# Two layers of a diffusion backbone on one core: another pattern of filler in layer 0's attention, and the first norm's sums between the halves of a modulation chunk

## The chip, the cores and the metric

The kernel runs on one core of one Trainium2 chip. The metric is the device time of one execution in microseconds (us). The time before is 1468.76 us, the median of three runs (1468.34 to 1469.26).

## The reference, cut to what matters

Two layers work on 512 latent tokens and, in layer 0, on 256 context tokens too; the width is 1024. In fp32:

```
for l in range(2):
    m = silu(cond) @ w_mod[l] + b_mod[l]          # six vectors of 1024 per stream: shift, scale, gate, twice
    h = rmsnorm(x, norm1_g[l]) * (1 + sc1) + sh1
    z = h @ w_in[l]                                # q (8 heads), k, v (2 heads of 64), u, g
    attn: softmax(q k^T) v; context sees context, latents see context and latents
    gm  = gelu(u) * (w_spatial @ layernorm(gelu(g)) + b)      # per group of 128 channels, chunks of 128 tokens
    x = x + ga1 * (concat(attn, gm) @ w_out[l])
    h2 = rmsnorm(x, norm2_g[l]) * (1 + sc2) + sh2
    x = x + ga2 * (relu(h2 @ w_ff1[l])**2 @ w_ff2[l])
```

The output is the latent stream alone.

## The kernel before, in words

Matrix products keep fp32 accuracy by a split: each operand is a high part (ACT, a cast, L226 for weights) and a low part (DVE, the difference, L231), and a product is three matmuls (L222). Activations lie transposed, channels on partitions. Weights come through a ring of buffers; `block_order()` fixes the order in which SP issues their loads: for layer 0 the modulation blocks `w_mod` (chunks 0 to 3 at the start, 4 to 11 during the attention, where high and low parts lie ready in memory) and the `w_out` blocks in the order in which the filler uses them.

**The start.** `start()` is scheduled in program order on PE and DVE. It computes the sum of squares of the latents (`lat.step`, the accumulate L498), modulation chunk 0 (16 matmuls in the trace, L373, from four loaded tiles, two per half), then `lat.sums`: the sums over partitions by matmuls with ones (L507), the scaling (L510), the power on POOL (L317), and the diagonal matrix of the result (L529). `fins.pop()()` picks the chunk's values out of its transpose (L381) by a selection matmul (L386) and stores them as shift and scale (L449, L452). `lat.bcast` spreads the norm over partitions (L534). Then the first half of chunk 1, then pieces of the normed input (L522 on DVE, L523 on ACT, L524 low part on DVE) and the first projection's main matmuls (L222).

**Layer 0's attention.** 16 tiles of the context and 32 of the latents run through one pipeline: scores (PE into `pa`), their maximum (DVE, L1052), the exponential (ACT, L1057), transposes of the weights (L1068 into `pt`) and their split (ACT L1070, DVE L1071), products with the values (PE into `pb`), the scaling, and mixing with the denominators (L1095 to L1101). The spatial mixing's matmuls (`pt<-ws,e` and `pt<-ws,acc`, L222, ended by L947 and L952) run among the context's tiles. A scheduler with costs of its own orders the rows of each engine inside this region. With each tile's step one **filler** is offered to TensorE: first the four halves of modulation chunks 4 and 5, then what the string FILL0 says. An "m" is half of a modulation chunk of 6 to 11, four matmuls that each use 32 of the 128 columns, so that four run side by side (L373). An "o" is a piece of the output projection's part from the spatial mixing, 12 matmuls of 128x384 (L222, `pb<-A,hi` and `pb<-A,lo`); the first "o" makes its operands (`make_gm`: ACT L812, DVE L814). A "." leaves the step without filler. When FILL0 is used up, 8 pieces of the output projection's attention part for the context follow, then 8 for the latents; the latter wait until all of the latents' tiles are done.

Of the kernel before, what the change touches and what calls it, by code (L numbers as in the profile page):

```python
# [8 lines left out]
F32 = mybir.dt.float32  # L9
# [3 lines left out]
ALU = mybir.AluOpType  # L13
# [100 lines left out]

FILL0 = "mmoooooooomomom.mom.mom.mom.mo.oo"
AB = ["A7", "A6", "A5", "A4"], ["B1", "B2", "B3", "B4"]
EARLY = AB[0] + ["B0"] + AB[1] + ["B5"] + AB[0] + ["B6"] + AB[1] + ["C0"]
PLAN = (("w0", "kv", "x0", "u1", "u2", "u3", "A0", "A1", "A2", "q", "B0", "B1", "B2"),  # L120
# [3 lines left out]
def block_order():  # L124
# [3 lines left out]
    for l in range(DEPTH):  # L128
# [17 lines left out]
        if l == 0:  # L146
            o += mod(4) + mod(5)
            rest = mod(6) + mod(7) + mod(8) + mod(9) + mod(10) + mod(11)
            n = 0
            for c in FILL0:  # L150
                if c == "m":
# [20 lines left out]
def trunk(ctx: ExitStack, tc: tile.TileContext, xT, pk1, pk2, rope, wsT, w_mod, w_tok, w_u, w_out, w_ff1, w_ff2, outT):  # L172
    nc = tc.nc
    vec, act, pe, pool_e = nc.vector, nc.scalar, nc.tensor, nc.gpsimd
# [46 lines left out]
    def mm(out, a, b, start, stop, n):  # L221
        pe.matmul(out, a, b, start=start, stop=stop)  # L222
        fl.vt += max(n / 2.4, 113.0) + 3.0

    def split(hi, lo, src, eng=None):
        act.copy(hi, src)  # L226
        if state.get("gated") and eng is vec and src.shape[-1] == 1024:
            for c in (slice(0, 512), slice(512, 1024)):
                vec.tensor_tensor(out=lo[:, c], in0=src[:, c], in1=hi[:, c].bitcast(F32), op=ALU.subtract)  # L229
            return  # L230
        (eng or vec).tensor_tensor(out=lo, in0=src, in1=hi.bitcast(F32), op=ALU.subtract)  # L231
# [8 lines left out]
    held, pend = [], []  # L240

    def convert():

        if held:
            split(*held.pop(0))

    def pump():
        while state["live"] < RING and state["pos"] < len(order):
# [111 lines left out]
    fins, mods = [], []  # L360

    def mod_chunk(l, j, lag=1200.0):


        ps = pb()
        ns = 4
        rows = ns * 32
        for kb in range(0, 4, ns // 2):
            ws_ = take("mod", l, j, kb) if j > 3 else (take("mod", l, j, kb)[0], take("mod", l, j, kb + 1)[0])
            for k2 in range(ns):  # L370
                k = kb * 2 + k2
                q = k2 * 32
                pe.matmul(ps[q:q + 32, :], S32[:, k, :], ws_[k2 // 2][:, k2 % 2 * 512:(k2 % 2 + 1) * 512], start=k < ns, stop=k >= KT - ns)  # L373
            fl.vt += PAR["MV"] * ns
            if j > 3:
                release()
            if kb < 4 - ns // 2:
                yield

        tr = (tw if l == 0 and j < 4 else tsm)([128, 512])  # L380
        vec.transpose(tr[0:rows], ps[0:rows])  # L381

        def fin():
            p4 = pt((128, 4, 2))
            for a in range(4):
                pe.matmul(p4[a * 32:a * 32 + 32], P1("sel")[0:rows], tr[0:rows].rearrange("p (m a i) -> p a m i", m=4, a=4)[:, a, :, 0:2], start=True, stop=True)  # L386
            if l == 0 and 0 < j < 4:
                mods.append(lambda: mod_store(l, j, p4))
            else:
                mod_store(l, j, p4)  # L390
        if lag is None:
            fins.append(fin)
        elif lag:
            fl.defer(lag, fin)
        else:
            fin()
        yield
# [65 lines left out]
    cx = kv0 = None  # L463
# [8 lines left out]
    def run(gen):  # L472
        for _ in gen:
            fl.tick()
# [231 lines left out]
    def layer(l, h, nxt, K, kv=None, kv0=0):  # L706
# [562 lines left out]
        def mixed(a, b):  # L1269
            for c in FILL0:  # L1270
                if c == ".":
                    yield "wait"
                else:
                    next(a if c == "o" else b)
                    yield
            yield from a
            yield from b
# [184 lines left out]
    def start():  # L1462
        chunk = [mod_chunk(0, c, None) for c in range(4)]
        for k in range(KT):
            lat.step(k)
        run(chunk[0])
        lat.sums(pool=1)
        fins.pop()()
        lat.bcast()
        next(chunk[1])  # L1470
        kvq = WideProj(h0)
        for c in range(4):
            k = 2 * c
            if c:
                convert()
                mods.pop()()
            lows = [lat.pieces(h0, k)]
            if not c:
                convert()
                lows.pop()()  # L1480
            lows.append(lat.pieces(h0, k + 1))
            for f in lows:
                f()
            if c == 2:
                for i in range(KT):
                    cx.step(i)
            if 0 < c < 3:
                run(chunk[c + 1])
            kvq.latents(k, cx.sums if c == 3 else fins.pop() if fins else None)
            if not c:  # L1490
                run(chunk[1])
            kvq.latents(k + 1, fins.pop() if fins else None)
        cx.bcast()
        return kvq
# [4 lines left out]
    lat, cx = Norm(0, 0, 0, 512, 0), Norm(0, 0, 512, 256, 1)  # L1499
    h0 = [unit(f"A{k}", [128, 2, T]) for k in range(8)]  # L1500
    with tc.manual_schedule(engines={ET.PE, ET.DVE}):
        kvq = start()
    while held:
        convert()
    held = None
# [63 lines left out]
```

## Time and profile before

| | |
|---|---|
| median of three runs | 1468.76 us (1468.34 to 1469.26) |
| profiled execution | 1468.59 us, its span 1466.8 us |
| granted TensorE clock, mean | 0.999 |
| TensorE busy | 1435.3 us, 98% |
| VectorE, ScalarE, GpSimd busy | 913.5, 639.8, 354.0 us |
| HBM | 145.26 MB read, 100 GB/s over the span |

Engines: PE is TensorE, PEld its weight loads, DVE VectorE, ACT ScalarE, POOL GpSimd, SP SyncE, which issues the DMAs. A row of the timeline is start, duration, engine, line, operation, output<-inputs, shape and count; in brackets stand the idle time of the engine before it and what ended that. A row of waits is engine, output and line, what was waited for, the total in us, how often, and the longest. Where stretches are listed, the columns are from:to, length, busy time and count of each engine named, granted clock, DMA share and GB/s. Busy TensorE time is modelled from pipelined matmuls, so it isn't TensorE at its peak.

### The profile page before, as it was taken

The page shows a single profiled execution, that of the slowest core. Times are in us where ns is not written, and L with a number is a line of the kernel's source. Part 1 is how long each engine was busy: PE and PEld are TensorE (multiplying, and loading weights), DVE is VectorE, ACT ScalarE, POOL GpSimd, SP SyncE. Part 2 cuts the span into 40 slices and gives each one's busy share as a digit, 9 for nine tenths or more (in the row PEclk, how much of TensorE's full clock was granted, in tenths as well). Part 3 has the DMA queues.
Part 4 walks back from the last instruction along what each step waited for, and adds up shares of the span by engine and source line. Part 5 has one row for each costly group of instructions (what it writes and reads, how often), then busy time and mean ns, then how long its engine had stood idle before and what let it go on. Part 6 is the DMA issues. An engine that isn't in the chain of part 4 may idle for free.

```text
span 1466.8 us, 21050 instructions
## 1 busy us (share of the span) xinstructions
PE 1435.3 (98%) x8178; PEld 1224.1 (83%) x8178; DVE 913.5 (62%) x1613; ACT 639.8 (44%) x1134; POOL 354.0 (24%) x304
## 2 busy tenths in 40 slices
PE   6999999999999999999999999999999999999998
PEld 2899787988888888888888889998989888888887
DVE  5857767777766565655556537778868554444443
ACT  3552546664545453433424234547755223332221
POOL 0333512222256461323233223142221000000000
PEclk9999999999999999999999999999999999999999
DMA  9322544101233343434343212210002323332331
GB/s 368 115 73 87 192 150 143 65 1 58 85 128 119 108 145 97 142 97 131 104 144 110 92 43 74 101 59 30 30 29 80 122 88 100 101 98 90 101 101 58
DMA packets 50084, 148.72 MB, mean 101 GB/s; under 512 B 5440, under 2 KB 6976, under 8 KB 49984
## 3 DMA queue, kind: packets, MB, share of 16 engines
q1 hardware_dynamic: 49408, 146.72, 30.0%
q8 instruction: 64, 1.05, 0.3%
q10 hardware_dynamic: 576, 0.66, 0.1%
q14 instruction: 36, 0.29, 0.1%
HBM read 145.26 MB, written 2.10 MB: 100 GB/s over the span
## 4 chain that ended last, share of the span: by engine, by line
PE 89%; DVE 6%; ACT 2%; DMA 1%; issue 1%; POOL 1%; SPq 0%; POOLq 0%; ACTq 0%; DVEq 0%
PE pa L222 55%; PE pb L222 25%; PE pt L222 2%; PE pb L373 2%; PE pt L1068 2%; PE pt L1192 1%; PE pt L764 1%; DMA A<-in_w_mod 1%; ACT hi L226 1%; DVE s L545 1%; DMA hi<-in_w_mod 0%; DVE A L541 0%; POOL m L317 0%; DVE X L1002 0%; DVE lo L229 0%
## 5 line engine op out<-in xcount | busy, mean ns | idle before, releaser
L222 PE MATMUL pa<-A,hi 128*128 128x512 f32 (+2 forms) x1440 | 429.7, 376 | 0.5 <-ACT hi L226 0.3
L226 ACT CAST hi<-raw 128x1024 fp32r<-128x1024 f32 x168 | 176.0, 1048 | 328.2 <-PE pa L222 242.0
L222 PEld LDWEIGHTS pa<-A,hi 128*128 128x128 f32 x1440 | 262.7, 188 | 46.7 <-ACT hi L226 0.5
L222 PE MATMUL pa<-A,lo 128*128 128x512 f32 (+2 forms) x832 | 283.9, 347 | 0.0
L231 DVE TENSOR_TENSOR lo<-raw,hi 128x1024 fp32r<-128x1024 f32 x144 | 191.4, 1329 | 119.6 <-ACT hi L226 115.8
L422 POOL TENSOR_TENSOR C<-C,s 128x512 f32<-128x512 f32 x112 | 175.4, 1581 | 293.9 <-ACT s L421 287.1
L222 PE MATMUL pa<-B,hi 128*128 128x512 f32 x750 | 239.0, 391 | 0.0
L222 PEld LDWEIGHTS pa<-A,lo 128*128 128x128 f32 x832 | 156.6, 188 | 21.6 <-DVE lo L229 0.2
L1002 DVE SCALAR_TENSOR_TENSOR X<-pa,modT,X 128x512 f32<-128x512 f32 x168 | 99.8, 615 | 106.5 <-PE pa L222 105.1
L222 PEld LDWEIGHTS pa<-B,hi 128*128 128x128 f32 x750 | 139.9, 188 | 27.1
L222 PE MATMUL pb<-B,hi 128*128 128x512 f32 (+1 forms) x600 | 156.8, 349 | 0.8 <-DVE mix L1224 0.7
L222 PE MATMUL pa<-B,lo 128*128 128x512 f32 (+1 forms) x450 | 155.2, 354 | 0.0
L1002 DVE SCALAR_TENSOR_TENSOR X<-pb,modT,X 128x512 f32<-128x512 f32 (+3 forms) x116 | 70.8, 619 | 76.9 <-PE pb L222 76.7
L222 PE MATMUL pb<-hi,A 128*128 128x256 f32 (+1 forms) x608 | 118.1, 291 | 0.6 <-DVE m L744 0.6
L222 PEld LDWEIGHTS pb<-B,hi 128*128 128x128 f32 x600 | 104.4, 189 | 15.5 <-DVE X L1002 0.9
L222 PE MATMUL pb<-B,lo 128*128 128x512 f32 (+1 forms) x300 | 104.1, 347 | 0.0
L222 PEld LDWEIGHTS pb<-hi,A 128*128 128x128 f32 x608 | 96.9, 191 | 2.2 <-PE pb L222 0.8
L222 PEld LDWEIGHTS pa<-B,lo 128*128 128x128 f32 x450 | 84.5, 188 | 14.9
L421 ACT ACTIVATE s<-k,silu 128x512 f32<-128x512 f32 x112 | 77.8, 717 | 36.6 <-DMA k<-in_w_mod 29.5
L222 PE MATMUL pb<-lo,A 128*128 128x256 f32 (+1 forms) x304 | 87.7, 289 | 0.0
L222 PE MATMUL pb<-A,hi 128*128 128x384 f32 (+2 forms) x288 | 81.1, 362 | 0.4 <-DVE mix L1099 0.3
L1399 DVE TENSOR_TENSOR w<-pa,w 128x256 f32<-128x256 f32 x28 | 11.9, 425 | 89.0 <-ACT w L1398 89.0
(230 smaller groups left out, 2250.0 us busy)
## 6 DMA issues: line engine op xcount, KB each, us to landing
raw<-in_w_ff SPq DMA_DIRECT2D x128, 512.0 KB, 3.5
k<-in_w_mod SPq DMA_DIRECT2D x96, 256.0 KB, 2.9
raw<-in_w_tok SPq DMA_DIRECT2D x16, 512.0 KB, 3.5
raw<-in_w_out SPq DMA_DIRECT2D x16, 512.0 KB, 3.5
lo<-in_w_mod SPq DMA_DIRECT2D x16, 512.0 KB, 4.5
hi<-in_w_mod SPq DMA_DIRECT2D x16, 512.0 KB, 4.3
A<-in_w_mod SPq DMA_DIRECT2D x8, 512.0 KB, 10.1
B<-in_w_mod SPq DMA_DIRECT2D x8, 512.0 KB, 9.4
```

The source lines that it names most:

```text
L222: pe.matmul(out, a, b, start=start, stop=stop)
L226: act.copy(hi, src)
L231: (eng or vec).tensor_tensor(out=lo, in0=src, in1=hi.bitcast(F32), op=ALU.subtract)
L373: pe.matmul(ps[q:q + 32, :], S32[:, k, :], ws_[k2 // 2][:, k2 % 2 * 512:(k2 % 2 + 1) * 512], start=k < ns, stop=k >= KT - ns)
L421: act.activation(p, w, AF.Copy, scale=s)
L422: pool_e.tensor_tensor(out=a, in0=a, in1=p, op=ALU.add)
L545: vec.scalar_tensor_tensor(out=t, in0=xk(k)[:, off:off + n], scalar=Amod[l][w][:, k, cond:cond + 1], in1=self.bc[:, 0:n], op0=ALU.mult, op ...
L764: pe.transpose(p[:, o:o + 128], stk[:, t, hh, c0:c0 + 128].bitcast(F32), ident)
L1002: vec.scalar_tensor_tensor(out=xs, in0=src[:, s - off:e - off], scalar=modT[l][:, i * 8 + m, cond:cond + 1], in1=xs, op0=ALU.mult, op1=ALU ...
L1068: pe.transpose(tp_[:, (kt - k0) * 128:(kt - k0) * 128 + 128], p[:, kt * 128:kt * 128 + 128], ident)
L1192: pe.transpose(tp_[:, kt * 128:kt * 128 + 128], p[:, (k0 + kt) * 128:(k0 + kt) * 128 + 128], ident)
L1399: vec.tensor_tensor(out=c, in0=ps[:, 512:768], in1=c, op=ALU.add)
```

## The change

FILL0 gets a new pattern: four halves of modulation chunks in front in place of two, 12 "m" and 16 "o" as before, and 8 pauses in place of 5, which lie from the middle on. With it the order of the loads changes. At the start, the norm's sums stand between the two halves of chunk 0; the broadcast stands ahead of the selection; the first half of chunk 1 moves behind the first main matmuls (it is handed to the first projection step as what runs between its two token tiles); and the first block's low part is converted in two halves of 512 columns.

```
-FILL0 = "mmoooooooomomom.mom.mom.mom.mo.oo"
+FILL0 = "mmmmooooo.oomo.mo.m.mom.mo.mo.moo.oo"
...
+    def convert_first():
+
+        hi, lo, raw = held.pop(0)
+        act.copy(hi, raw)
+
+        def low(c):
+            vec.tensor_tensor(out=lo[:, c], in0=raw[:, c], in1=hi[:, c].bitcast(F32), op=ALU.subtract)
+        low(slice(0, 512))
+        return lambda: low(slice(512, 1024))
...
+        next(chunk[0])
+        lat.sums(pool=1)
         run(chunk[0])
-        lat.sums(pool=1)
+        lat.bcast()
         fins.pop()()
-        lat.bcast()
-        next(chunk[1])
         kvq = WideProj(h0)
...
             if not c:
-                convert()
+                later = convert_first()
                 lows.pop()()
             lows.append(lat.pieces(h0, k + 1))
+            if not c:
+                later()
...
-            kvq.latents(k, cx.sums if c == 3 else fins.pop() if fins else None)
+            kvq.latents(k, cx.sums if c == 3 else fins.pop() if fins else (lambda: next(chunk[1])) if not c else None)
```

In the changed kernel the lines behind `convert_first` have numbers larger by 10 (L373 is L383, L386 is L396, L507 is L517, L534 is L544, L1068 is L1078).

TensorE at the start of the program, before: chunk 0 (`pb<-A`), sums, selection, broadcast, chunk 1's first half (`pb<-B`), main matmuls.

```order
L373 MATMUL pb_208<-A_8_101,S_88 32x512 x2
L373 MATMUL pb_208<-A_9_103,S_88 32x512 x2
L507 MATMUL pt_219<-ones,acc_50_185 128x1 x4
L386 MATMUL pt_230<-w_217,c_70 32x8 x4
L534 MATMUL pt_237<-c_70,w_228 128x128 x4
L373 MATMUL pb_242<-B_13_109,S_88 32x512 x2
L373 MATMUL pb_242<-B_14_111,S_88 32x512 x2
L222 MATMUL pa_247<-hi_107,A_42_175 128x512
```

And in the change:

```order
L383 MATMUL pb_208<-A_7_99,S_88 32x512 x2
L517 MATMUL pt_213<-ones,acc_50_185 128x1 x4
L383 MATMUL pb_208<-A_8_101,S_88 32x512 x2
L383 MATMUL pb_208<-A_9_103,S_88 32x512 x2
L544 MATMUL pt_230<-c_70,w_222 128x128 x4
L396 MATMUL pt_235<-w_228,c_70 32x8 x4
L222 MATMUL pa_242<-hi_107,A_42_175 128x512
L222 MATMUL pa_242<-lo_108,A_42_175 128x512
L222 MATMUL pa_242<-hi_107,A_42_175 128x512 x2
L222 MATMUL pa_242<-lo_108,A_42_175 128x512
L222 MATMUL pa_242<-hi_107,A_42_175 128x512
L383 MATMUL pb_261<-B_13_109,S_88 32x512 x2
```

The sums moved ahead of the second half of chunk 0, the broadcast ahead of the selection, and chunk 1's half behind six main matmuls.

VectorE at the same place, before (L381 the transpose of chunk 0, L529 the diagonal):

```order
L381 STREAM_TRANSPOSE w_217<-pb_208 128x512
L510 TENSOR_SCALAR m_224<-pt_219 128x4
L529 COPY w_228<-m_226 128x512
L449 TENSOR_TENSOR modT_90<-pt_230,c_70 128x2x4
L452 SCALAR_TENSOR_TENSOR A_92<-modT_90,c_70 128x4
```

And in the change:

```order
L520 TENSOR_SCALAR m_218<-pt_213 128x4
L539 COPY w_222<-m_220 128x512
L391 STREAM_TRANSPOSE w_228<-pb_208 128x512
L459 TENSOR_TENSOR modT_90<-pt_235,c_70 128x2x4
L462 SCALAR_TENSOR_TENSOR A_92<-modT_90,c_70 128x4
```

The transpose now stands behind the diagonal.

TensorE among the context's tiles, before (L373 halves of modulation chunks, L1068 transposes, `pa<-B,B` scores):

```order
L222 MATMUL pa_1879<-B_98_480,B_117_566 128x256
L373 MATMUL pb_1886<-hi_1591,S_88 32x512 x2
L373 MATMUL pb_1886<-lo_1592,S_88 32x512 x2
L373 MATMUL pb_1886<-hi_1843,S_88 32x512
L1068 MATMUL pt_1874<-c_70,w_1860 128x128 x2
L386 MATMUL pt_1891<-s_1866,c_70 32x8 x4
```

And in the change:

```order
L222 MATMUL pa_1878<-B_98_481,B_117_567 128x256
L383 MATMUL pb_1885<-hi_1592,S_88 32x512
L1078 MATMUL pt_1873<-c_70,w_1861 128x128 x2
L383 MATMUL pb_1885<-hi_1592,S_88 32x512
L383 MATMUL pb_1885<-lo_1593,S_88 32x512 x2
L396 MATMUL pt_1890<-s_1867,c_70 32x8 x4
L222 MATMUL pa_1907<-B_97_480,B_117_567 128x256
L222 MATMUL pa_1907<-B_98_481,B_117_567 128x256
L383 MATMUL pb_1885<-hi_1844,S_88 32x512
L1078 MATMUL pt_1902<-c_70,w_1883 128x128 x2
```

A half whose first matmul stands apart from its other three is called split here. In the order of the whole attention 5 halves of 16 are split before (2 among the context's tiles, 3 among the latents'), and 9 in the change (4 and 5).

## The prediction

> **What bounds the kernel now.** I read the page first, then the busy time by stage, then the waits of the stage that changes, then the first 28 us instruction by instruction.
>
> ```profile
> PE 1435.3 (98%) x8178; PEld 1224.1 (83%) x8178; DVE 913.5 (62%) x1613; ACT 639.8 (44%) x1134; POOL 354.0 (24%) x304
> PE 89%; DVE 6%; ACT 2%; DMA 1%; issue 1%; POOL 1%; SPq 0%; POOLq 0%; ACTq 0%; DVEq 0%
> ```
>
> TensorE is busy for 98% of the span and is 89% of the chain that ended last. So the time is TensorE's own work plus its few holes, and a change counts by what it does to either. The busy time of TensorE by stage (us from:to, length, busy, matmuls, granted clock, DMA share, GB/s):
>
> ```profile
> 0.00:24.00 24.00, 10.08 (x46) 0.93 0.94 351
> 24.00:160.00 136.00, 134.76 (x918) 1.00 0.33 115
> 160.00:190.00 30.00, 26.36 (x202) 1.00 0.75 258
> 190.00:300.00 110.00, 110.00 (x777) 1.00 0.31 108
> 300.00:330.00 30.00, 28.19 (x216) 1.00 0.01 2
> 330.00:1467.00 1137.00, 1125.91 (x6030) 1.00 0.28 92
> ```
>
> The changed pattern orders 160 to 330: 160 to 190 are the context's attention tiles with their spatial mixing, 190 to 300 the latents' tiles with filler, 300 to 330 the last tiles. The holes there are 3.64, 0 and 1.81 us. Who ended them:
>
> ```profile
> PE pt L386 <- DVE s L947: 1.3, 1, 1.3
> PE pt L1068 <- DVE A L1071: 1.2, 2, 0.8
> PE pt L222 <- DVE acc L231: 1.2, 1, 1.2
> PE pb L222 <- ACT A L1070: 0.6, 2, 0.4
> PE pt L1068 <- DVE modT L456: 0.6, 1, 0.6
> PE pb L222 <- DVE mix L1099: 0.3, 1, 0.3
> PE pb L373 <- DMA hi<-in_w_mod: 0.2, 1, 0.2
> ```
>
> The L1071 and L1070 rows are the bare last tiles (1.8 us together); the other five are the context stage (3.6 us). So no edit of the filler can win more than 5.4 us, and whatever it adds to TensorE in the full middle is paid in full.
>
> **The change part by part.** First the **start**, whose order in the trace of before is:
>
> ```profile
> 12.12 5.33 PE L373 MATMUL pb<-A,S 128*32 128x512 f32 x16 [12.12 <-DMA A<-in_w_mod]
> 17.39 1.05 PE L507 MATMUL pt<-ones,acc 128*128 128x1 f32 x8
> 17.51 0.72 DVE L381 STREAM_TRANSPOSE w<-pb 128x512 f32<-128x512 f32 x1 [4.14 <-PE pb L373]
> 18.37 0.25 PE L386 MATMUL pt<-w,c 128*32 128x8 f32 x8
> 18.79 1.02 POOL L317 TENSOR_TENSOR m<-m,mhalf 128x4 f32<-128x4 f32 x1 [17.81 <-DVE m L510]
> 19.84 0.43 DVE L529 COPY w<-m 128x512 f32<-128x512 f32 x1 [1.20 <-POOL m L317]
> 20.18 0.16 DVE L449 TENSOR_TENSOR modT<-pt,c 128x8 f32<-128x8 f32 x1
> 20.38 0.17 DVE L452 SCALAR_TENSOR_TENSOR A<-modT,c 128x4 f32<-128x4 f32 x1
> 20.41 1.09 PE L534 MATMUL pt<-c,w 128*128 128x128 f32 x4 [1.80 <-DVE modT L449]
> 21.43 1.94 PE L373 MATMUL pb<-B,S 128*32 128x512 f32 x8
> 21.54 0.75 DVE L522 SCALAR_TENSOR_TENSOR s<-X,A,pt 128x512 f32<-128x512 f32 x1 [1.00 <-PE pt L534]
> 23.30 0.73 PE L222 MATMUL pa<-hi,A 128*128 128x512 f32 x1
> 26.63 1.07 PE L373 MATMUL pb<-B,S 128*32 128x512 f32 x8
> ```
>
> Before, the sums (L507) follow the whole chunk 0; the square root on POOL, the diagonal (L529) and the broadcast (L534) come last, and the first main matmul starts at 23.30, 1.76 after the first scaled piece (L522, 21.54). Now the sums come behind half the chunk, that is about 12.12 + 5.33/2 = 14.8. They took 1.05; so early, with the first chunk's 16 matmuls at 0.33 us each against 0.13 in the row at 26.63, I allow twice that: 16.9. From the end of the sums (18.44) to the end of the diagonal (20.27) it was 1.83, so the diagonal ends at 18.7. The other half chunk, 1.07 to 1.94, ends between 18.0 and 18.8; the transpose now stands behind the diagonal on DVE and ends at 0.72 after the later, 19.5. Selection 0.25, L449 0.16, L452 0.17 and about 0.2 of handovers give 20.3 for L522, plus 1.76 the first main matmul at 22.1: 1.2 us earlier. Bounds: 2.3 earlier if the sums keep 1.05 and all slides with them, 0 if the later second half eats it.
>
> But chunk 1's first half stood at 21.43, between broadcast and first main matmul, where TensorE waited for DVE and ACT in any case. It now stands inside the first projection step, with nothing to hide it: 8 matmuls, +1.07 by the row at 26.63. (The two DMAs that its buffers hold back come some 2 us later; the queue still has work, and TensorE's stage from 24 to 160 has only 1.24 us of holes of all kinds, so I put that at 0, at most 1.) The conversion in two halves lets the scaled piece's low part in between; it costs one more DVE start, hidden by ACT's part. 0.
>
> The half chunk also kept TensorE busy ahead of the main matmuls. The clock:
>
> ```profile
> 17.00:20.40 3.40, 1.62 (x18) 1.14 (x17) 1.41 (x5) 1.04 (x1) 1.02 (x1) 1.00 1.03 410
> 20.40:23.80 3.40, 3.38 (x13) 1.40 (x14) 2.40 (x4) 0.72 (x1) 0.00 (x0) 0.50 1.03 411
> ```
>
> A stretch with 1.62 of 3.40 us busy was followed by one at a granted 0.50, and the stretch of 3.38 busy by full clock. In the change 20.4 to 23.8 holds TensorE work from 22.1 only, 1.7 of 3.4, so I expect the next 3.4 us, all main matmuls, at 0.50. Eight matmuls took 1.94 there against 1.07, a loss of 45%: 3.4 x 0.45 = +1.5; at best 0, at worst a second part-stretch, 1.7 x 0.45 = 0.8 more. **Start: -1.2 + 1.07 + 1.5 = +1.4** (-1.2 to +4.4).
>
> The Trainium skill (TensorE: Matmul & The Clock Gate, Part 1: The HAM clock gate) says that the clock is halved by default, that about 3.4 us of sustained activity lift it, and that the window is free-running, so its phase differs from run to run. The stretches above agree on the length; that the phase differs no run shows yet. By that rule the loss here would be anything from 0 to 1.5 with the phase, the sum 1469.9 to 1471.4, and repeated runs of the change would scatter by it.
>
> **The filler: split halves.** Half a modulation chunk is four matmuls on four column groups (two of the high, two of the low part), each two records in the trace. Kept together, all four run side by side; where the scheduler puts other rows behind the first, it runs alone:
>
> ```profile
> 166.66 0.62 PE L373 MATMUL pb<-hi,S 128*32 128x512 f32 x2
> 167.66 0.51 PE L222 MATMUL pa<-B,B 128*128 128x256 f32 x2
> 210.74 1.04 PE L373 MATMUL pb<-hi,S 128*32 128x512 f32 x2
> 211.72 0.62 PE L222 MATMUL pb<-A,hi 128*128 128x384 f32 x2
> 215.18 0.62 PE L373 MATMUL pb<-hi,S 128*32 128x512 f32 x1
> 216.17 0.96 PE L222 MATMUL pa<-B,B 128*128 128x512 f32 x4
> ```
>
> A whole half takes 166.66 to 167.66, 1.00. A split one takes 210.74 to 211.72 and again 215.18 to 216.17: 0.98 + 0.99. So a split costs 0.97. In the order of before 5 halves are split, 2 in the context's stage and 3 among the latents; in the changed order 9, 4 and 5. **Context +1.94, latents +1.94.** The latter has no hole to hide in (110.00 of 110.00). Lower bound of the first: 0, if the singles only fill waits.
>
> **The context's waits.** With four halves in front and dense pieces later, the waits for L947 (1.3), the accumulate L231 (1.2), L456 and the mix lose their place, since DVE gains about 2 us on TensorE: -3.6 at most. New ones arise. The transposes behind the first split wait for the exponentials (I take 0.6, like the L456 row); those behind the accumulate take 0 to 0.9; and the first dense pieces now stand right behind the last spatial mix, whose product must still go through DVE:
>
> ```profile
> 187.44 0.69 DVE L952 TENSOR_TENSOR C<-s,C 128x512 f32<-128x512 f32 x1
> 189.08 1.83 DVE L814 TENSOR_TENSOR A<-C,A 128x768 fp32r<-128x768 f32 x2
> ```
>
> From product to usable low part that is 0.69 + 0.92 and ACT's copy between, against some single rows of scores, values and transposes as cover; I take 1.6 (0.5 to 3.3). New waits 2.6, so **-1.0** (-3.1 to +0.6).
>
> **Pauses and end.** Before, 37 fillers ran ahead of the 8 output pieces and the last three of 48 tiles were bare; now 40 do, and each of the last 8 tiles has a piece of 12 matmuls. That takes the 1.8 of L1071 and L1070: **-1.8** (at least -0.8, if half of it returns). The three new pauses leave tiles bare in the full middle; those before left no hole there, so **+0.3**, at most 1.5, the price of a bare tile or two at the end (0.8 each at the longest).
>
> Sum: 1.4 + 1.94 + 1.94 - 1.0 - 1.8 + 0.3 = **+2.8 us**. The profiled execution took 1468.59 (span 1466.8 and 1.8 around it), so **1471.4**; the median of the runs shown, 1468.76, is 0.17 above that execution, well under the uncertainty of a term.
>
> **Rivals.** (a) The clock doesn't drop: the start is then -1.2 + 1.07 and the sum +1.3, 1469.9. For it: broadcast and selection fall into the stretch too, and TensorE may count as busy. Against: the 1.62 row. (b) Faster, by one mechanism in the context's stage: TensorE's extra second there is just what DVE lacked, so no wait returns and the two splits run inside what were holes. Then 3.6 goes and the 1.94 is not paid: 0 + 1.94 - 3.6 - 1.8 + 0 with an even start = -3.5, 1465.1. It decides once the new waits stay under about 0.3 us in all. For it: all five waits there are on DVE or a load and none on TensorE's own rows; against: DVE is already busy for most of that stage, and the dense piece directly behind the mix. (c) DMA becomes the bound in front: each half takes two loads of this kind,
>
> ```profile
> hi<-in_w_mod SPq DMA_DIRECT2D x16, 512.0 KB, 4.3
> ```
>
> so 1 MB, 4 us at the stage's 258 GB/s, and eight halves now follow each other where six did; one of them already waited for a load. If one misses its place by three quarters of that, 3.1 is added: 1474.5. Against: that wait was 0.2 and the loads run ahead through dense work. (d) The splits don't cost what they did, since neighbours fill them: the sum without 3.9 is -1.1, 1467.5; the rows at 210.74 and 215.18 speak against it.
>
> **How the numbers follow.** The forecast (1469.9 to 1473.5 as its own range) has 0.55; (a) 0.15, (b) 0.12, (c) 0.08, (d) 0.10. A change below 0.2%, 2.9 us, can't be told from none here. Faster by more: (b), 0.12. Slower by more than 2.9: (c) and half of the forecast, whose middle lies at 2.8: 0.36. The rest, 0.52, is within. The range leaves out half of (b) below and the upper end of (c): 1466.0 to 1474.8.
>
> **What would show it.** Right: the first main matmul near 22, half a chunk within the first projection step, and a granted 0.50 over the main matmuls after 23.8; nine places with L373 alone for 0.97; the L947 and L231 waits gone and one before a 128x384 dense matmul on L812 or L814; no wait for L1071 or L1070 after 300. Wrong: TensorE's busy time from 160 to 330 not some 4 us larger, full clock at the start, or waits for w_mod loads over 1 us in the context's stage.

## The result and the profile after

The changed kernel takes 1477.96 us, the median of four runs (1475.83 to 1479.09), against 1468.55 for the kernel before on the same chip: a ratio of 1.006 (95% interval 1.0048 to 1.0073), 9.4 us slower. The prediction was 1471.4 with a range to 1474.8. The profiled execution took 1476.86, its span 1475.0. Where an execution ran in the chip's slower state, as one of the eleven of e7_cover_dve did (1776.71 us at a granted clock of 0.754), it is left out of the medians below.

Where the time arises can be read from one and the same matmul in both traces. First the first filler of the attention, from the two timelines, before and after:

```profile
163.71 0.62 PE L373 MATMUL pb<-hi,S 128*32 128x512 f32 x2
```

```profile
166.12 0.62 PE L383 MATMUL pb<-hi,S 128*32 128x512 f32 x2
```

Then the first broadcast of the second norm, just behind the attention, as the group of its line (nanoseconds of one, first and last start):

```profile
L534 PE MATMUL pt<-c,w x2: 273/273/273, 339.2 to 339.3; 128*128 128x128 f32 x2
```

```profile
L544 PE MATMUL pt<-c,w x2: 272/272/272, 347.4 to 347.5; 128*128 128x128 f32 x2
```

So 2.4 us are lost before 166, 5.8 between there and 347, and the span as a whole is 8.2 longer: nothing more is lost behind the attention. (The medians differ by 9.4; the trace shows one execution.) The start of the changed kernel, TensorE alone:

```profile
15.06 1.87 PE L517 MATMUL pt<-ones,acc 128*128 128x1 f32 x8
16.86 1.93 PE L383 MATMUL pb<-A,S 128*32 128x512 f32 x8
18.82 1.11 PE L544 MATMUL pt<-c,w 128*128 128x128 f32 x4
22.18 0.79 PE L222 MATMUL pa<-hi,A 128*128 128x512 f32 x1 [2.03 <-ACT A L533]
25.04 1.94 PE L383 MATMUL pb<-B,S 128*32 128x512 f32 x8
26.91 0.80 PE L222 MATMUL pa<-hi,A 128*128 128x512 f32 x1
```

The first main matmul starts at 22.18 in place of 23.30, as forecast (22.1). But chunk 1's half takes 1.94 inside the projection, where 1.07 was expected, and the matmuls up to 27.9 run at that pace: 5.7 us at half speed and not 3.4. The column of the granted clock, which prints 1.00 here until the first change of the clock is recorded at 27.9, doesn't show it; the durations do.

The waits of TensorE between 160 and 345:

```profile
PE pb L222 <- DVE A L824: 2.1, 1, 2.1
PE pb L222 <- ACT A L822: 1.4, 1, 1.4
PE pb L383 <- DVE s L391: 1.4, 1, 1.4
PE pt L1078 <- ACT w L1067: 0.8, 2, 0.5
PE pt L1078 <- DVE A L1081: 0.7, 1, 0.7
PE pb L222 <- POOL B L231: 0.2, 1, 0.2
```

The old holes (L947, L231, L456, L1099) are gone, as forecast, and new ones of 5.7 us stand in their place among the context's tiles where 3.6 stood; the last two rows are the end, 0.9 in place of 1.8. Behind the three largest stand GpSimd, VectorE beside it, and a load. First the two scalings of before, then the rows of the changed kernel:

```profile
179.32 1.11 DVE L922 TENSOR_SCALAR s<-s,mv,m 128x128 f32<-128x128 f32 x4
```

```profile
180.18 4.68 POOL L231 TENSOR_TENSOR lo<-raw,hi 128x1024 fp32r<-128x1024 f32 x2
181.29 3.66 DVE L932 TENSOR_SCALAR s<-s,mv,m 128x128 f32<-128x128 f32 x2
184.87 0.70 DVE L391 STREAM_TRANSPOSE s<-pb 128x512 f32<-128x512 f32 x1
193.97 1.05 ACT L226 CAST hi<-raw 128x1024 fp32r<-128x1024 f32 x1 [2.43 <-DMA raw<-in_w_out]
195.09 2.35 POOL L231 TENSOR_TENSOR lo<-raw,hi 128x1024 fp32r<-128x1024 f32 x1 [4.40 <-ACT hi L226]
195.78 3.35 DVE L824 TENSOR_TENSOR A<-C,A 128x768 fp32r<-128x768 f32 x2 [0.85 <-ACT A L822]
```

GpSimd takes the low part of a `w_out` block in 2.35 us. Two scalings of 128x128 on VectorE, where four took 1.11 us before, take 3.66 and end 0.1 us after GpSimd's two conversions (184.86). The dense pieces' two low parts, 1.83 in the row quoted in the prediction, take 3.35; the first alone takes 2.48 and ends 0.8 us after GpSimd's conversion, which is about its own length (0.92). TensorE waits for both: through the transpose behind the scalings (L391), and directly for the low parts.

ACT's wait of 1.4 us comes from a load. ACT had nothing to do for 2.43 us, until a `w_out` block landed; it cast the block from 193.97 on and came to the dense operands (L822) at 194.92, though they had been ready since 193.85 (the end of L962 on VectorE). The load of this block, the third, was issued at 187.57, with six halves' `w_mod` loads of FILL0 in front of it. In the kernel before there are three in front, and it was issued 14 us earlier:

```profile
173.29 1.50 SPq L273 DMA_DIRECT2D raw<-in_w_out  x2
```

The same late load sets GpSimd's conversion at 195.09, beside the low parts.

And the clock, in stretches of 3.4 us:

```profile
191.70:195.10 3.40, 2.67 (x27) 1.00 0.85 309
195.10:198.50 3.40, 0.63 (x2) 1.00 0.16 60
198.60:201.90 3.30, 3.30 (x14) 0.50 0.46 146
```

After the stretch with 0.63 us of work the next 3.4 are granted half speed: by the prediction's 45%, an estimated 1.5 us more.

### The profile page after: what moved, and what is told of

It reads as the page before. It is cut to its first block, busy times and chain, and to the rows that moved or that the text cites. A ratio compares the mean times of both kernels' runs of the same rounds, so it can differ in the third digit from the quotient of the medians.

```text
span 1475.0 us, 21057 instructions
## 1 busy us (share of the span) xinstructions
PE 1441.8 (98%) x8178; PEld 1227.4 (83%) x8178; DVE 919.7 (62%) x1614; ACT 640.6 (43%) x1134; POOL 354.0 (24%) x304
## 4 chain that ended last, share of the span: by engine, by line
PE 87%; DVE 7%; ACT 2%; issue 1%; POOL 1%; DMA 1%; SPq 0%; POOLq 0%; ACTq 0%; DVEq 0%
PE pa L222 55%; PE pb L222 23%; PE pt L222 2%; PE pb L383 2%; PE pt L1078 2%; PE pt L1202 1%; PE pt L774 1%; ACT hi L226 1%; POOL m L327 1%; DMA A<-in_w_mod 1%; DVE lo L231 0%; DVE s L555 0%; DMA lo<-in_w_mod 0%; DVE A L551 0%; DVE s L932 0%
## 5 line engine op out<-in xcount | busy, mean ns | idle before, releaser
L231 DVE TENSOR_TENSOR lo<-raw,hi 128x1024 fp32r<-128x1024 f32 x144 | 194.8, 1353 | 120.0 <-ACT hi L226 115.8
```

## The experiments

Each ratio is to the kernel before on the same chip.

**The start alone and the filler alone.** Two kernels, each with one part of the change.

```
e1_start: the changed kernel with FILL0 = "mmoooooooomomom.mom.mom.mom.mo.oo"
e2_fill:  the kernel before with FILL0 = "mmmmooooo.oomo.mo.m.mom.mo.mo.moo.oo"
```

> Only the start edit, the old FILL0. In the changed kernel's trace the first main matmul starts 1.1 us earlier, but a matmul of the first projection is 2.4 us later from 26 us on, and the clock is full only from 27.9. Clock theory (the quiet ahead of the main matmuls lets TensorE run them at half clock): +1 to +4 us against before, about +2.4, with runs that differ by up to 2 or 3 us. Rival, work only (the half chunk's 1.07 us against the 1.1 won, the clock of that one execution being chance): within 0.5 us of before. Either way the attention's holes stay those of before.

> Only the new FILL0, the old start. Theory (the two edits add up): +5.7 us against before, the difference that the changed kernel's trace gathers between 168 and 334 us: +3 by split halves, +2 by holes among the context's tiles, +1.5 by a stretch at half clock behind the holes, -0.9 at the end. Rival (the late start shifts loads against the attention and makes its holes): +1 to +3 us.

The start alone: 1470.68 us, 1.0013 (1.0005 to 1.0022), +2.2 by the medians. The filler alone: 1475.11, 1.0045 (1.0032 to 1.0058), +6.7. Together 8.9 of the 9.4: the parts add up, and the filler's loss doesn't hang on the start. In the trace of the start alone the first filler starts at 166.04, 2.3 us later than before; 0.6 of that lies ahead of everything that the edit moves, in the first load (first matmul at 12.75, before at 12.12). There half speed lay on 24.0 to 27.4, 3.4 us as forecast. In the filler's trace the holes are those of the changed kernel but for ACT's, 2.2 in place of 1.4, and the clock is lower for two stretches:

```profile
190.90:194.30 3.40, 1.17 (x9) 1.00 0.49 169
194.40:197.70 3.30, 1.22 (x5) 0.50 0.31 78
197.80:201.20 3.40, 3.40 (x15) 0.50 0.17 70
```

Two stretches with little work are followed by two at half speed here; in the changed kernel's execution it was one of each.

**The start with its cover.** Chunk 1's half goes back to where TensorE has nothing else to do.

```
 (e1_start)
         lat.bcast()
         fins.pop()()
+        next(chunk[1])
         kvq = WideProj(h0)
...
-            kvq.latents(k, cx.sums if c == 3 else fins.pop() if fins else (lambda: next(chunk[1])) if not c else None)
+            kvq.latents(k, cx.sums if c == 3 else fins.pop() if fins else None)
```

> The start edit with the old FILL0, but the first half of chunk 1 stands again between the selection and the first main matmul. Clock theory: TensorE stays busy there, the main matmuls get full clock about as early as before, and the 1.1 us from the sums stay: -1 us against before (-1.5 to 0), 3 us under the start edit. Rival, work only: the half chunk is out of the path again, so also -1; but then the start edit is at 0, and the two differ by 1 us.

1468.24 us, 0.9998 (0.9989 to 1.0007): 2.4 us under the start edit alone, where 1.07 of matmuls had been moved. In the traces the first filler starts at 162.00 here and at 166.04 there; of these 4.0 us 1.07 are the moved work and 0.55 the later first load, which leaves 2.4. So work only, which gave 1 us between the two, falls; the clock, which gave 3, holds.

```profile
19.06 1.77 PE L383 MATMUL pb<-B,S 128*32 128x512 f32 x8
21.25 0.50 PE L222 MATMUL pa<-hi,A 128*128 128x512 f32 x1 [0.42 <-ACT A L533]
24.53 1.07 PE L383 MATMUL pb<-B,S 128*32 128x512 f32 x8
```

The main matmuls start at 21.25, at full speed (0.50 for one, 1.07 for the half chunk). But 1 us faster than before was expected, and 0.2 came. That is only partly explained. In this execution (1467.24) the first filler starts 1.7 us earlier than before, and the granted clock of the context's stage, 160 to 190, is 0.94 against 1.00 before. The four kernels traced with the early sums and the old front (e1, e3, e7, e10) all show 0.89 to 0.94 there, and the four traced with the old start and the old front (before, e5, e6, e9) 1.00. Why was not tried.

**VectorE in place of GpSimd.**

```
 (e2_fill)
-            eng = pool_e if "%s%d" % key[:2] in PAR["WP"] and key[:3] != ("out", 1, 0) else vec
+            eng = pool_e if "%s%d" % key[:2] in PAR["WP"] and key[:3] not in (("out", 1, 0), ("out", 0, 0)) else vec
```

> The new FILL0 with the old start, and the low parts of the four w_out blocks of the dense pieces taken on VectorE in place of GpSimd. 7 split halves in place of 9 by the order, worth -1.9 us. Port theory (VectorE's instructions with two inputs in SBUF wait until GpSimd's 2.35 us conversions end; that makes the 1.4 and 2.1 us holes and, by them, the half-clock stretch): those holes and the stretch go, -4 to -5 us more, so about 6 us under the new FILL0 alone and near before. Rival (the holes come from the dense piece standing right behind the mix, whoever converts): only the -1.9, or worse by the 1.2 us that each conversion adds on VectorE.

1469.68 us, 1.0008 (0.9999 to 1.0017): 5.4 under the filler alone, 6 expected. Of the waits of this kernel the largest and the two for the dense operands, and then the two groups of VectorE that had been stretched:

```profile
PE pt L1068 <- ACT w L1057: 1.9, 4, 0.8
PE pb L222 <- ACT A L812: 0.6, 1, 0.6
PE pb L222 <- DVE A L814: 0.6, 1, 0.6
```

```profile
181.41 0.58 DVE L922 TENSOR_SCALAR s<-s,mv,m 128x128 f32<-128x128 f32 x2
191.95 1.82 DVE L814 TENSOR_TENSOR A<-C,A 128x768 fp32r<-128x768 f32 x2
```

The two scalings take 0.58 and the two low parts 1.82; the wait for L381 is gone. Of the 5.4 us about 2 go to two split halves fewer (L373's busy time falls from 25.76 to 23.53), the rest to the holes and the clock behind them. That GpSimd's conversions stretch VectorE's instructions holds. Not all that was expected came: the wait for the exponentials (L1057) grew from 0.8 to 1.9, and the half clock did not go, but fell from 6.8 us to 3.4:

```profile
190.00:300.00 110.00, 108.44 (x740) 0.98 0.29 98
```

The edit also moved a load: the third `w_out` block was issued at 181.30, with the filler alone at 185.01, and its cast ran at 186.84, long before the dense operands. So ACT's wait, 2.2 with the filler alone and 0.6 here, fell with the earlier load; how much of the gain is the load's and how much VectorE's this run doesn't separate.

**Split halves.** The first matmul of each half is handed out one filler earlier.

```
 (the kernel before, mod_chunk, for chunks 6 to 11)
+                if apart and k2 == 0:
+                    yield
 (mixed, behind each filler)
+                if FILL0[i + 1:i + 2] == "m":
+                    next(b)
```

> The kernel before, with the first matmul of each half of chunks 6 to 11 handed out one filler earlier than the other three: 12 split halves in place of 5 by the order, nothing else meant to change. Split theory (a lone matmul takes 0.97 us and TensorE is full there): +6.8 us, 0.97 for each of the 7. Rival (the neighbours run beside it or the time is found again in a later wait): less than +2.

1474.48 us, 1.0041 (1.0027 to 1.0055): +6.2 for 7 splits, 0.89 each, and no new stretch at half clock in its trace. L373's busy time within 160 to 345, before and with the halves apart (then, for the changed kernel, L383's):

```profile
160.00:345.00 185.00, 22.22 (x128) 1.00 0.32 109
```

```profile
160.00:345.00 185.00, 28.28 (x128) 1.00 0.32 108
```

```profile
160.00:345.00 185.00, 25.75 (x128) 0.99 0.31 107
```

The same 128 matmuls take 22.22, 28.28 and 25.75. The change's four further splits cost 3.5.

**Pauses alone and front alone.**

```
e6_pauses: the kernel before with FILL0 = "mmoooooooomo.mom.mo.m.mom.mo.m.mo.oo"
e11_front: the kernel before with FILL0 = "mmmmooooooomo.mo.m.mom.mo.momoooo"
```

> The kernel before with three more pauses from the middle on and its old front (two halves, then dense pieces): FILL0 = mmoooooooomo.mom.mo.m.mom.mo.m.mo.oo. 8 split halves in place of 5 by the order, +2.9; the waits at the bare last tiles fall from 1.8 to about 0.7, -1.1. Theory (the front makes the new holes, the pauses only the splits): +1.8 us, no waits for the dense pieces' operands and no half clock in the latents' stage. Rival (the pauses in the middle make the holes): +4 or more.

> The kernel before with the new front alone: FILL0 = mmmmooooooomo.mo.m.mom.mo.momoooo, 5 pauses as before and the last three tiles bare as before; 6 split halves in place of 5. Theory (the front makes the holes and the half clock): the waits for the dense pieces' operands (2 x 2 us) and for L381 (1.4) are there, +2 by holes, +1.5 to +3 by the clock, +1 by the split: +4.5 to +6. Rival (the new pauses make them): +1 to +2.

Pauses: 1470.94 us, 1.0018 (1.0008 to 1.0027), +2.7 where 1.8 was expected, and none of the new holes; L373's busy time rose by 3.0 (25.24 for 22.22), which covers the loss. Front: 1473.39, 1.0035 (1.0021 to 1.0048), +4.9, with them all:

```profile
PE pb L222 <- ACT A L812: 3.2, 1, 3.2
PE pb L222 <- DVE A L814: 1.8, 1, 1.8
PE pb L373 <- DVE s L381: 1.4, 1, 1.4
```

So the front makes the holes, the pauses don't.

**Two combinations that don't beat the kernel before.** The kept half and VectorE's conversion, with the old and with the new FILL0.

```
e7_cover_dve:     e3_cover with the line of e4_dve
e8_cover_dve_new: the same with FILL0 = "mmmmooooo.oomo.mo.m.mom.mo.mo.moo.oo"
```

> The old FILL0, the early sums with chunk 1's half kept ahead of the main matmuls, and the w_out low parts of the dense pieces on VectorE. 5 split halves as before. If the start's 2.1 us hold and the accumulate's 1.2 us wait for GpSimd goes: -3 us against before (-4 to -1.5). Rival (VectorE, with 4.8 us more to do, holds TensorE up elsewhere, or the clock falls in the context's stage as it did in the one execution with the half kept): -1 to +1.

> As the run just told, with the new FILL0: 7 split halves, pieces beside all of the last tiles. If the parts add up: the new FILL0 with VectorE's conversion measured +1.2 us, the start with the half kept -0.2, so +1.0 (-1 to +3), and 8 us under the changed kernel. Rival (the clock's windows decide, and the early start shifts them): anything from -2 to +4 by execution.

With the old FILL0 1470.46 us, 1.002 (1.001 to 1.0029): 2.2 slower, where 3 faster was expected, and beyond the rival too. The context's stage of this kernel:

```profile
160.00:190.00 30.00, 26.86 (x189) 0.89 0.71 252
```

TensorE is busy 26.86 us there, 0.5 more than before (26.36), and yet behind: half clock fell on it from 183.5 on for 6.8 us. The wait for the accumulate is gone, but one of 1.7 us for ACT's cast in front of it has come. VectorE's conversion helped the new front and harmed the old one in these runs. With the new FILL0 1468.60 us, 1.0001 (0.9992 to 1.001): +0.3, where +1.0 was expected; 9.1 under the changed kernel, each taken against the kernel before on its own chip.

**Fewer splits.** From the price of a split it follows that a pattern with the old front, 8 pauses and only 3 splits should win.

```
e9_three:        the kernel before with FILL0 = "mmoooooooom.om.ommom.m.o.mmomm.o.o.o"
e10_three_cover: e3_cover with the same FILL0
```

> The kernel before with FILL0 = mmoooooooom.om.ommom.m.o.mmomm.o.o.o: the old front, 8 pauses, 3 split halves in place of 5 by the order and pieces beside nearly all of the last tiles. If a split is worth 0.97 us and the bare last tiles 1.1: -3.0 us against before. Rival (the three new bare tiles in the full middle cost what the end gives back, as the 0.9 us by which the run with pauses missed its sum may say): -1.0 to -2.0.

> The same FILL0 with the early sums and chunk 1's half kept ahead of the main matmuls. If the parts add up: 0.2 under the run before it by the medians, so about -3.2 us against before; if the start's 2.1 us by the trace come through now, -5. Rival (the context's holes, which are those of before, fall together with a half-clock stretch as in the trace of the half kept): within 1 us of before's time less 3.

1465.36 us, 0.998 (0.9971 to 0.9989), -3.2; and with the start edit and its cover 1464.48, 0.9973 (0.9962 to 0.9983), -4.0: both beat both kernels. Of the first one's waits, those at the end are down to 0.2:

```profile
PE pb L222 <- ACT A L1070: 0.2, 1, 0.2
```

So the bare last tiles and two splits are worth what the traces said, and three more bare tiles in the full middle cost nothing that shows.

## Why the prediction was wrong

By its own terms, the sum of +2.8 against the 8.2 of the profiled executions:

| term | predicted | found | by |
|---|---|---|---|
| start: sums earlier, half chunk moved | -1.2 + 1.07 | -1.1 + 1.07 | timeline |
| start: clock | +1.5 | +2.4 | what is left of the 2.4 lost by 166 |
| split halves | +3.9 | +3.5 | L383's busy time |
| context's waits | -1.0 | +2.1 | waits, 5.7 in place of 3.6 |
| half clock behind the new holes | not in the sum | +1.5 (estimate) | clock's stretches |
| bare last tiles | -1.8 | -0.9 | waits |
| new bare tiles | +0.3 | about 0 | the pattern with three splits |

The found terms add up to 8.6, 0.4 more than the whole: they are taken from views of different kinds (waits, busy time, clock), which overlap a little.

**The steps that failed** are "The context's waits" and, with it, a term that wasn't there. I took the dense operands' chain as 0.69 + 0.92 and a copy, from rows in which GpSimd stood still, and gave VectorE its usual durations and ACT a free start. In the changed order 1.6 became 3.5: 2.1 for the low parts, which met GpSimd's conversion and waited it out, and 1.4 for ACT's copy, which stood behind the cast of a block that had landed late. (The term's range was also too short: by its own bounds its upper end is 0.6 + 0.9 + 3.3 - 3.6 = +1.2, not +0.6; the +2.1 found lies beyond both.) The warning of the first part stood in the trace of before: the accumulate that TensorE waited for by 1.2 us, at the time of a conversion.

```profile
181.26 2.39 POOL L231 TENSOR_TENSOR lo<-raw,hi 128x1024 fp32r<-128x1024 f32 x1 [2.68 <-PE pt L1068]
182.21 1.99 DVE L231 TENSOR_TENSOR acc<-s,e 128x512 fp32r<-128x512 f32 x1
```

The same 128x512 instruction takes 0.69 or less when GpSimd is idle (0.66 in the changed kernel). I read 1.99 as its length, not as a wait. The Trainium skill (SBUF — State Buffer, SBUF: two separate sides) states it: a VectorE instruction in a two-port mode, or one with two inputs in SBUF beside a GpSimd instruction that reads SBUF, needs a pair of ports that GpSimd uses too, and whichever starts later is blocked until the other's instruction is over. The rows agree: the two-input instructions end 0.55 and 0.82 us after GpSimd's, which is about their own length (0.66 and 0.92).

**The missed term.** I reckoned with half clock at the start, where the fence showed it, and not among the context's tiles, though I had put 2.6 us of waits there. Whoever expects waits of some 3 us within one stretch of 3.4 has to add the price of the next, at least as a chance. At the start the step was right in kind and too small: 5.7 us at half speed in place of 3.4 in this execution.

**The transposes of a modulation chunk (L381)** as a wait weren't foreseen at all: with four halves in front, a chunk's first half waits until VectorE has read the chunk before out of the same bank, and VectorE was held by GpSimd.

**What was right:** the first main matmul (22.18 for 22.1), the half chunk's price, the price and number of the splits (0.89 to 0.97; the rival that they cost nothing falls), the old waits' end, and the loss at the start by the clock, in kind if not in size. Rival (a), full clock at the start, falls with the 2.4 us that the cover brought back. Rival (c), the loads in front, came in another shape: TensorE never waited for a load of `w_mod` in the attention, but the `w_out` load queued behind them came late, and ACT waited 2.43 us for it. Rival (b), no new waits, was the opposite of what came.

**ACT's wait** varies with that load. In the three traces with the new front and GpSimd's conversions (the changed kernel, the filler alone, the front alone) ACT comes from the cast of the block to the dense operands 1.07, 1.87 and 2.87 us after they were ready, and TensorE waits 1.43, 2.23 and 3.24. **Left open:** why the landing itself varies (6.4, 7.2 and 8.2 us from issue to cast), and how the loss divides between the load and GpSimd, since no run moved the load alone.

## What to carry to other kernels

Before a duration from a trace is carried to another place in the order, look at what GpSimd does at the same time, there and here: a VectorE instruction that takes several times its usual length (here 2.48 for 0.92) can be a wait in disguise, and an order that moves it beside a long GpSimd instruction brings the wait along. Look, too, at what stands in front of it on its engine, and whether that waits for a load that the new order issues later. On an engine that is busy for 98%, count the groups of matmuls that a new order tears apart, since each lone one is paid in full; it is a number that the order alone gives. And a hole may not be over when the work goes on: here stretches of 3.4 us with 0.6 to 1.2 us of work were each followed by 3.4 us at half speed.

## What the runs showed of the hardware that was not expected

The clock's stretches have no fixed place in the program. The recorded changes lie at 17.0, 20.4 and 23.8 in the execution of before, at 27.9 in the changed one, and at 15.7 in that with the kept half, which had full clock from there through the start. In the seven traced kernels with the old start the first change lies anywhere from 15.3 to 17.8. The spread of one kernel's runs goes with the clock: of 27 runs of the kernel before (1467.04 to 1469.98) the four with a mean granted clock of 1.000 took at most 1467.86, the three with 0.996 or 0.997 at least 1469.36. This agrees with the free-running window of the Trainium skill (TensorE: Matmul & The Clock Gate, Part 1: The HAM clock gate).

Busy time alone doesn't say what the clock does next. In the same start, 1.62 of 3.4 us of work was followed by half clock in the execution of before (17.0 to 20.4) and by full clock in that with three splits (19.1 to 22.5).

Nor does everything that counts as busy in the profile lift the clock. The first stretches of the changed kernel, cut at its own window's edges:

```profile
14.20:17.70 3.50, 3.50 (x16) 1.00 1.02 408
17.70:21.10 3.40, 2.44 (x20) 1.00 1.03 410
```

TensorE has no hole in the first, 1.87 us of it the sums' matmuls of one column, and yet the matmuls behind it run at half speed (the second half of chunk 0 takes 1.93, the broadcast 1.11); in the kernel with the kept half a stretch full of chunk 0's 512-column matmuls was followed by full speed at 15.7. Whether the one-column matmuls are the cause was not tried.
